# z in the order q, k, v, with q and k normalised behind products, and w_out and b1 prepared on other engines

## The chip, the cores and the metric

One core of a Trainium2 chip runs the whole layer in one launch. The metric is the device time of that launch in microseconds. The engines named below are TensorE (PE, with its weight loads as PEld), VectorE (DVE), ScalarE (ACT), GpSimd (POOL) and SyncE (SP, which here issues most of the loads).

## What is computed

One hybrid layer on 512 tokens of width 1024. A projection `z = h @ w_in` feeds three branches, and a mixture of experts follows. Cut to what the change touches:

```python
h = rms_norm(x, norm1_g) * (1 + sc1) + sh1
z = h @ w_in
xr, xg, q, k, v, qi, ki, wi = jnp.split(z, ...)
y_rnn = rg_lru_branch(xr, xg, ...)                 # conv, gates, scan, gelu(xg) * h
q = rms_norm(q.reshape(B, S, 8, 64), q_norm_g)     # each head by itself
k = rms_norm(k.reshape(B, S, 8, 64), k_norm_g)
y_attn = dsa_attention(q, k, v, qi, ki, wi)        # indexer scores, top keys, softmax, product with v
mix = jnp.concatenate([rms_norm(y_rnn, rg_out_g), rms_norm(y_attn, attn_out_g)], -1) @ w_out
x = x + g1 * mix
h2 = rms_norm(x, norm2_g) * (1 + sc2) + sh2
x = x + g2 * moe_ffn(h2, ...)                      # top 4 of 32 experts; u = h2 @ w1[e] + b1[e], then w2[e]
```

All weights are float32. Each expert has 1024 x 2048 numbers in w1 and 1024 x 1024 in w2.

## The kernel before, in words

Dense products of float32 are made of three passes: an operand is split into a high part (ScalarE casts it to the reduced format, L152) and a low part (VectorE or POOL subtracts the high part, L153), and TensorE adds high x high, low x high and high x low (L157 to L159). A matrix of w_in is loaded in eight row blocks of 512 columns; `halves` splits and multiplies it in two halves. The last argument of `halves` and `tok_piece` is the engine that makes the low parts, VectorE if none is given. A product of four groups of tokens gives 24 records of 256 columns a group; two PSUM banks take turns, and ScalarE empties each (L293 for token-major results, L306 for xg).

The order of the stages around the change is: xr and xg of the recurrent branch, whose gates and four scans over 512 tokens run on ScalarE, POOL and VectorE (L399 a square root, L402, L403 the scan, L400 gelu, L404); k; k's norm (squares on ScalarE L454, sums L455, the inverse root by twelve small VectorE instructions, L141 to L148); v; `prep_k` (L462 scales k by its norm, L468 transposes it); w_out's first half with `split_out` (L491 multiplies its rows by g1r, the gate of the residual; L492 and L493 make high and low parts); q; the first four of eight products of the recurrent branch with w_out (`rg`); q's norm and `prep_q` (L553 scales, L475 transposes); then `attend`, four blocks of queries with pieces of other work handed in `between`. While VectorE still picks the top keys in rounds of two instructions (L361, L362), the z products run. The bias b1 of the experts is split into three parts of bf16 after `attend(3)`, on POOL (L680 to L686), for a product with one row that adds it in the expert stage. Behind attention and the second half of w_out the router sorts tokens, and a loop over experts streams w1 and w2 (1 MB a load, L823) from HBM, multiplies (L884, L911) and adds the rows to the output.

Memory is laid out by hand: R[0] to R[5] are regions of on-chip memory that weights, then other data, take in turn, so a load waits until the last reader of the region is done. Each engine runs its own list of instructions in order. Who comes first on each list is not written by hand: a list scheduler sorts the instructions by its own estimates of durations, once, when the kernel is built. The source order sets priorities.

Of the kernel before, what the change touches and what calls it, by code (L numbers as in the profile page):

```python
# [9 lines left out]
F32R = mybir.dt.float32r  # L10
BF = mybir.dt.bfloat16
# [26 lines left out]
def layer(ctx, tc, x, c, w_ada, b_ada, norm1_g, w_in, conv_w, conv_b, w_rg_a, b_rg_a, w_rg_x, b_rg_x,  # L38
# [148 lines left out]
    def load_in(kb, c0, n=512):  # L187
        return pair(kb, KD, n, 2, lambda t, ks: nc.sync.dma_start(t, wi_v[:, ks, c0:c0 + n]))
# [95 lines left out]
    def halves(piece, t, evac, sub=None):  # L284
        for a in range(2):
            piece(part_of(t, 256 * a, 256 * a + 256), *evac(a), sub)
# [149 lines left out]
    load_bd()  # L436
    w_xg = load_in(R[2], 512)
    halves(ch_piece, w_xr, lambda a: (ev_xr, 2 * a), G)
    w_k = load_in(R[0], 1536)
    modulate(1)  # L440
    for b in range(4):
        rg_in(b)
    halves(ch_piece, w_xg, lambda a: (ev_xg, 2 * a), G)
    rg_out()
    w_v = load_in(R[1], 2048, 256)
    dump("gx", gx)
    dump("xr", xrp)
    dump("yR", yR)
# [37 lines left out]
    def split_out(a, kb, g):  # L486

        raw, low = wo[a]
        hi = mem(kb, 4, D, dt=F32R)
        for b in range(4):  # L490
            G.tensor_mul(raw[b][:, 0], raw[b][:, 0], g1r)  # L491
            A.activation(hi[:, b], raw[b][:, 0], AF.Copy, scale=g(b))  # L492
            V.scalar_tensor_tensor(low[b][:, 0], raw[b][:, 0], g(b), hi[:, b], op0=OP.mult, op1=OP.subtract)  # L493
        return hi, [v[:, 0] for v in low]

    ssA = const.tile([128, NT], F32)
    mh, ml = mem(R[3] + 8, 4, S, dt=F32R), mem(R[4], 4, S, dt=F32R)

    def rg_half():
        p = bank(7)  # L500
        sq = mem(R[4] + 8, 4, S)
        for b in range(4):
            A.activation(sq[:, b], yR[:, b], AF.Square)
            T.matmul(p[32 * b:32 * b + 32, :], ones, sq[:, b], start=True, stop=True)
        V.tensor_copy(sq[:, 0], p)
        p = bank(7)
        for i in range(NT):
            T.matmul(p[:, i:i + 1], sq[:, 0, i * 128:(i + 1) * 128], fold[:, 0:1], start=True, stop=True)
        V.tensor_copy(ssA, p[:, 0:NT])
        r = rstd_of(ssA, 512, "rs1")  # L510
        for b in range(4):
            hilo(mh[:, b], ml[:, b], yR[:, b])
        wh, wl = split_out(0, R[1], grg)
        return r, wh, wl

    def rg_out_half(i, n, r, wh, wl):
        p = bank(0, 1, 2, 3)
# [3 lines left out]
            mm3(p, mh[:, b, sl], ml[:, b, sl], wh[:, b, ns], wl[b][:, ns], b, 4)  # L521
        V.scalar_tensor_tensor(part[:, i, ns], p, r[:, i:i + 1], part[:, i, ns], op0=OP.mult, op1=OP.add)  # L522


    halves(tok_piece, w_k, lambda a: (ev_tok(zk, 256 * a),), G)
    rk = norm_heads(zk, "k", 191, rls)
    tok_piece(w_v, ev_tok(zv, 0))
    for pr in range(4):
        prep_k(pr, rk)
    w_q = load_in(R[2], 1024)  # L530
    wo_v = w_out[0].rearrange("(b p) n -> p b n", p=128)
    wo = [None, None]

    def load_wo(a):
        wo[a] = pair(R[2 * a], 4, D, 1, lambda t, bs: nc.sync.dma_start(t, wo_v[:, 4 * a + bs.start:4 * a + bs.stop]))

    load_wo(0)
    rows_of(g1r, 0)
    brt = const.tile([128, E], F32)
    nc.sync.dma_start(brt, at(b_router, 0, [[0, 128], [1, E]]))  # L540
    nc.sync.dma_start(wrt, w_router[0].rearrange("(p k) e -> p k e", k=KD))
    half_a = rg_half()
    halves(tok_piece, w_q, lambda a: (ev_tok(zq, 256 * a),))
    for i in range(NT):
        nc.sync.dma_start(part[:, i], x[0, i * 128:(i + 1) * 128, :])
    load_wo(1)
    rg = [partial(rg_out_half, i, n, *half_a) for i in (3, 2, 1, 0) for n in range(2)]
    for f in rg[0:4]:
        f()
    rq = norm_heads(zq, "q", 191.5, [mem(174.75 + 2 * j, S) for j in range(2)])  # L550
    for i in range(NT):
        z = zq[:, i].rearrange("p (h d) -> p h d", h=H)
        (G if i % 2 else V).tensor_mul(z, z, rq[:, i, :, None].to_broadcast([128, H, HD]))  # L553
    for pr in range(4):
        prep_q(pr)


    natt = [0]
# [50 lines left out]
    def mix_in(i):  # L609

        y = yB[:, i]
        ssB = const.tile([128, 1], F32, name="ssB", tag="ssB", bufs=2)
        A.activation(sqB, y, AF.Square, accum_out=ssB)
        r = rstd_of(ssB, 512, "rB")
        bh, bl = [mem(R[3] + 2 * j, 4, 128, dt=F32R) for j in range(2)]
        p = bank(4, 5).rearrange("p (b t) -> p b t", b=4)
        for b in range(4):
            T.transpose(p[:, b], y[:, b * 128:(b + 1) * 128], ident)
        hilo(bh, bl, p)
        return bh, bl, r  # L620
# [48 lines left out]
    V.tensor_sub(upto_me, onesb, later)  # L669
    attend(3, rg[4:6])  # L670
    half_b = split_out(1, R[5], gat)

    b1t = const.tile([96, 2 * FF], BF)
    for n in range(2):
        ns = slice(n * FF, (n + 1) * FF)
        b1f = mem(R[3] + 4, FF)
        for j in range(3):
            nc.sync.dma_start(b1f[32 * j:32 * j + 32], b1[0, :, ns])
        b1o = b1f[0:96].rearrange("p (f two) -> p f two", two=2)[:, :, 1]
        G.tensor_scalar(b1o, b1o, 1.0, None, op0=OP.add)  # L680
        G.tensor_copy(b1t[:, ns], b1f[0:96])
        for j in range(1, 3):
            for q in range(j, 3):
                c = slice(32 * q, 32 * q + 32)
                G.tensor_sub(b1f[c], b1f[c], b1t[c, ns])
                G.tensor_copy(b1t[c, ns], b1f[c])  # L686
    m3 = mix_in(3)
    attend(2, rg[6:7] + [partial(mix_half, 3, n, *m3, *half_b) for n in range(2)])
    m2 = mix_in(2)
# [395 lines left out]
```

## Time and profile before

| | us |
|---|---|
| median of 3 runs | 1457.71 (1455.44 to 1466.08) |
| profiled execution | 1457.75 |
| its span on the core | 1455.9 |
| TensorE busy | 1363.4, 94% of the span |
| VectorE busy | 547.6, 38% |
| ScalarE busy | 273.3, 19% |
| POOL busy | 204.1, 14% |
| HBM moved | 482.39 MB |

The span is what the hardware profiler saw of the core's instructions; the time of the execution is 1.85 us longer. The granted clock of TensorE is given as a share of full speed, 2.4 GHz; the other level is 1.2 GHz, 0.50. Matmuls are pipelined: a record's duration is longer than the distance to the next. An idle time in brackets stands ahead of an instruction, with what ended it.

### The profile page before, as it was taken

To read this page: it belongs to the slowest core of one execution; us is meant where nothing else is said; L and a number is where in the kernel's file an instruction comes from. 1 tells how busy PE (TensorE), PEld (TensorE's weight loads), DVE (VectorE), ACT (ScalarE), POOL (GpSimd) and SP (SyncE) were. 2 spreads that over 40 slices of the span, in tenths; PEclk is the share of its full clock that TensorE was granted. 3 is DMA by queue.
4 is the path that set the end of the run, shared out by engine and by line. 5 is a ranking of instruction groups with operands and counts; after the bars stand their busy time and mean duration, and the time that the engine had idled before them with its cause. 6 is when DMAs were issued, how large, how long until landed. Compare 5 with 4: busy or idle time off the path is not lost. (4 is left out here: it accounts for less than half of the span.)

```text
span 1455.9 us, 26502 instructions
## 1 busy us (share of the span) xinstructions
PE 1363.4 (94%) x10907; PEld 611.4 (42%) x10907; DVE 547.6 (38%) x1317; ACT 273.3 (19%) x552; POOL 204.1 (14%) x238
## 2 busy tenths in 40 slices
PE   5999988999799999999999999999999999999993
PEld 2854887767533343334333333333333333333320
DVE  4579986755722222214212231223132122212221
ACT  4445553433111100101011000001010010100100
POOL 4312623511100010000001011000000000100000
PEclk9999999878689999999999999999999999999997
DMA  9676113014999999999999999999999999999995
GB/s 373 219 270 231 59 59 117 22 58 159 374 390 363 323 404 392 391 407 404 409 395 403 418 401 383 402 410 389 410 399 404 409 405 407 399 393 393 395 418 197
DMA packets 83398, 482.39 MB, mean 331 GB/s; under 512 B 11778, under 2 KB 14018, under 8 KB 33098
## 3 DMA queue, kind: packets, MB, share of 16 engines
q1 hardware_dynamic: 75034, 453.88, 77.8%
q0 software_dynamic: 7520, 24.68, 6.7%
q8 instruction: 87, 1.43, 0.4%
q10 hardware_dynamic: 720, 2.10, 0.4%
q14 instruction: 37, 0.30, 0.1%
HBM read 465.14 MB, written 15.48 MB: 330 GB/s over the span
## 5 line engine op out<-in xcount | busy, mean ns | idle before, releaser
L884 PE MATMUL bank<-mem,mem 128*32 128x512 f32 x5504 | 622.4, 595 | 0.0
L884 PEld LDWEIGHTS bank<-mem,mem 128*32 128x32 f32 x5504 | 174.6, 110 | 371.6 <-issue 363.2
L911 PE MATMUL bank<-mem,mem 128*32 128x512 f32 x2304 | 268.4, 593 | 0.0
L889 DVE TENSOR_TENSOR bank<-bank,mem 128x512 f32<-128x512 f32 x86 | 60.0, 697 | 410.1 <-PE bank L884 409.8
L911 PEld LDWEIGHTS bank<-mem,mem 128*32 128x32 f32 x2304 | 85.0, 110 | 146.0 <-issue 134.1
L891 ACT ACTIVATE mem<-bank 128x256 f32<-128x256 f32 x86 | 33.1, 385 | 527.8 <-DVE bank L889 527.8
L930 DVE SCALAR_TENSOR_TENSOR mem<-bank,gate_h,mem 64x512 f32<-64x512 f32 x72 | 54.0, 749 | 207.2 <-PE bank L911 206.5
L933 POOL DMA_INDIRECT out_dram<-mem,idx_all x32 | 47.0, 1470 | 581.7 <-DVE mem L930 525.9
L157 PE MATMUL bank<-mem,mem 128*128 128x512 f32 (+1 forms) x320 | 115.0, 362 | 2.9 <-DVE mem L522 2.3
L158 PE MATMUL bank<-mem,mem 128*128 128x512 f32 (+1 forms) x320 | 113.7, 355 | 0.0
L159 PE MATMUL bank<-mem,mem 128*128 128x512 f32 (+1 forms) x320 | 112.7, 352 | 0.0
L855 POOL DMA_INDIRECT mem<-h_d,idx_all x32 | 30.2, 943 | 400.4 <-PE bank L863 342.7
L157 PEld LDWEIGHTS bank<-mem,mem 128*128 128x128 f32 x320 | 62.3, 196 | 14.3 <-issue 3.5
L159 PEld LDWEIGHTS bank<-mem,mem 128*128 128x128 f32 x320 | 62.4, 195 | 12.9 <-issue 6.8
L917 PE MATMUL bank<-mem,mem 128*32 128x512 f32 x448 | 61.8, 601 | 6.0 <-SPq L1014 4.3
L158 PEld LDWEIGHTS bank<-mem,mem 128*128 128x128 f32 x320 | 62.6, 195 | 9.3 <-issue 3.5
L864 DVE COPY mem<-bank 128x512 f32<-128x512 f32 (+2 forms) x32 | 18.0, 564 | 112.5 <-PE bank L863 112.2
L863 PEld LDWEIGHTS bank<-ident,mem 128*128 128x128 f32 (+2 forms) x256 | 33.7, 196 | 58.7 <-issue 26.8
L902 ACT COPY mem<-bank 128x512 f32<-128x512 f32 (+1 forms) x32 | 18.3, 573 | 207.9 <-PE bank L911 115.3
L863 PE MATMUL bank<-ident,mem 128*128 128x128 f32 (+2 forms) x256 | 43.6, 295 | 11.2 <-ACT mem L902 5.1
L153 POOL TENSOR_TENSOR mem<-mem,mem 128x512 fp32r<-128x512 f32 (+1 forms) x28 | 41.2, 1490 | 86.4 <-ACT mem L152 86.3
L901 PEld LDWEIGHTS bank<-ident,mem 128*128 128x128 f32 x172 | 24.5, 207 | 37.5 <-issue 21.1
(325 smaller groups left out, 1216.9 us busy)
## 6 DMA issues: line engine op xcount, KB each, us to landing
mem<-in_w_dram SPq DMA_DIRECT2D x384, 1024.0 KB, 15.1
mem<-in_w_ada_dram SPq DMA_DIRECT2D x24, 1024.0 KB, 6.3
mem<-in_w_in_dram SPq DMA_DIRECT2D x20, 512.0 KB, 5.5
mem<-in_x_dram SPq DMA_DIRECT2D x8, 512.0 KB, 6.4
mem<-in_w_out_dram SPq DMA_DIRECT2D x8, 512.0 KB
mem<-in_w_in_dram SPq DMA_DIRECT2D x8, 256.0 KB, 5.9
mem<-mod_d SPq DMA_DIRECT2D x4, 512.0 KB, 6.0
h_d<-mem POOLq DMA_DIRECT2D x4, 512.0 KB, 8.6
```

What stands on the lines that cost most here:

```text
L153: (sub or V).tensor_sub(lo, src, hi)
L157: T.matmul(p, ah, bh, start=(k == 0), stop=False)
L158: T.matmul(p, al, bh, start=False, stop=False)
L159: T.matmul(p, ah, bl, start=False, stop=(k == n - 1))
L863: T.transpose(p[:, k, 0:n], xgs[frm][0:n, 4 * q + k::KD], ident[0:n, 0:n])
L884: T.matmul(bk[b][32 * n:32 * n + 32, :], xT[:, k, BT * b:BT * b + BT], w[k][:, 0, n * 512:(n + 1) * 512], start=(k == 0), stop=(k == KD - 1))
L889: V.tensor_add(bk[b], bk[b], biasb[j % 2])
L891: A.activation(act[:, b], u[:, :, 0], AF.Gelu_apprx_sigmoid)
L911: T.matmul(bk[6 + b // 2][o:o + 32, :], aT[:, b, c, BT * n:BT * n + BT], w[n][:, c, m * 512:(m + 1) * 512], start=(n + c == 0), stop=(n == ...
L917: T.matmul(bk[6 + nb // 2][o:o + 32, :], aT[:, nb - 1, c, BT * n:BT * n + BT], w[n][:, c, m * 512:(m + 1) * 512], start=(n == 0), stop=(n ...
L930: V.scalar_tensor_tensor(ys[64 * h:64 * h + a.stop - a.start, ns], p[a], gate_h[a, h, j:j + 1], g2h[a], op0=OP.mult, op1=OP.mult)
L933: G.indirect_dma_start(out=out_rows, out_offset=bass.IndirectOffsetOnAxis(ap=idx_all[a, j:j + 1], axis=0), in_=ys[a], in_offset=None, comp ...
```

## The change

Four things are altered. The z products come in the order q, k, v: w_q takes R[0], w_k R[1] and w_v R[2], and POOL makes the low parts of all three. q's norm and its product with z follow q's product, all on VectorE; k's product is cut in two halves, with `prep_q` and the recurrent branch's sums of squares around its second half; k's norm stands ahead of v's product, and `prep_k` behind it. In `split_out` the rows of w_out are multiplied by g1r on VectorE in place of POOL. And b1 is split ahead of k's norm by `split_b1`, with VectorE and ScalarE, in a piece of memory of its own; `mh` and the buffers `bh`, `bl` change places in R[3].

```diff
--- before.py
+++ after.py
@@ -436,13 +436,14 @@
     load_bd()
     w_xg = load_in(R[2], 512)
     halves(ch_piece, w_xr, lambda a: (ev_xr, 2 * a), G)
-    w_k = load_in(R[0], 1536)
+    w_q = load_in(R[0], 1024)
     modulate(1)
     for b in range(4):
         rg_in(b)
+    w_k = load_in(R[1], 1536)
     halves(ch_piece, w_xg, lambda a: (ev_xg, 2 * a), G)
     rg_out()
-    w_v = load_in(R[1], 2048, 256)
+    w_v = load_in(R[2], 2048, 256)
     dump("gx", gx)
     dump("xr", xrp)
     dump("yR", yR)
@@ -488,13 +489,13 @@
         raw, low = wo[a]
         hi = mem(kb, 4, D, dt=F32R)
         for b in range(4):
-            G.tensor_mul(raw[b][:, 0], raw[b][:, 0], g1r)
+            V.tensor_mul(raw[b][:, 0], raw[b][:, 0], g1r)
             A.activation(hi[:, b], raw[b][:, 0], AF.Copy, scale=g(b))
             V.scalar_tensor_tensor(low[b][:, 0], raw[b][:, 0], g(b), hi[:, b], op0=OP.mult, op1=OP.subtract)
         return hi, [v[:, 0] for v in low]
 
     ssA = const.tile([128, NT], F32)
-    mh, ml = mem(R[3] + 8, 4, S, dt=F32R), mem(R[4], 4, S, dt=F32R)
+    mh, ml = mem(R[3], 4, S, dt=F32R), mem(R[4], 4, S, dt=F32R)
 
     def rg_half():
         p = bank(7)
@@ -510,8 +511,7 @@
         r = rstd_of(ssA, 512, "rs1")
         for b in range(4):
             hilo(mh[:, b], ml[:, b], yR[:, b])
-        wh, wl = split_out(0, R[1], grg)
-        return r, wh, wl
+        return r
 
     def rg_out_half(i, n, r, wh, wl):
         p = bank(0, 1, 2, 3)
@@ -521,38 +521,61 @@
             mm3(p, mh[:, b, sl], ml[:, b, sl], wh[:, b, ns], wl[b][:, ns], b, 4)
         V.scalar_tensor_tensor(part[:, i, ns], p, r[:, i:i + 1], part[:, i, ns], op0=OP.mult, op1=OP.add)
 
-
-    halves(tok_piece, w_k, lambda a: (ev_tok(zk, 256 * a),), G)
-    rk = norm_heads(zk, "k", 191, rls)
-    tok_piece(w_v, ev_tok(zv, 0))
-    for pr in range(4):
-        prep_k(pr, rk)
-    w_q = load_in(R[2], 1024)
+    b1t = const.tile([96, 2 * FF], BF)
+
+    def split_b1():
+
+        for n in range(2):
+            ns = slice(n * FF, (n + 1) * FF)
+            b1f = mem(161.75, FF)
+            for j in range(3):
+                nc.sync.dma_start(b1f[32 * j:32 * j + 32], b1[0, :, ns])
+            b1o = b1f[0:96].rearrange("p (f two) -> p f two", two=2)[:, :, 1]
+            V.tensor_scalar(b1o, b1o, 1.0, None, op0=OP.add)
+            A.copy(b1t[:, ns], b1f[0:96])
+            V.tensor_sub(b1f[0:96], b1f[0:96], b1t[:, ns])
+            for q in (1, 2):
+                c = slice(32 * q, 32 * q + 32)
+                A.copy(b1t[c, ns], b1f[c])
+            V.tensor_sub(b1f[64:96], b1f[64:96], b1t[64:96, ns])
+            A.copy(b1t[64:96, ns], b1f[64:96])
+
+
     wo_v = w_out[0].rearrange("(b p) n -> p b n", p=128)
     wo = [None, None]
 
     def load_wo(a):
         wo[a] = pair(R[2 * a], 4, D, 1, lambda t, bs: nc.sync.dma_start(t, wo_v[:, 4 * a + bs.start:4 * a + bs.stop]))
 
-    load_wo(0)
+
+    halves(tok_piece, w_q, lambda a: (ev_tok(zq, 256 * a),), G)
     rows_of(g1r, 0)
     brt = const.tile([128, E], F32)
     nc.sync.dma_start(brt, at(b_router, 0, [[0, 128], [1, E]]))
     nc.sync.dma_start(wrt, w_router[0].rearrange("(p k) e -> p k e", k=KD))
-    half_a = rg_half()
-    halves(tok_piece, w_q, lambda a: (ev_tok(zq, 256 * a),))
+    load_wo(0)
+    rq = norm_heads(zq, "q", 191.5, rls)
+    for i in range(NT):
+        z = zq[:, i].rearrange("p (h d) -> p h d", h=H)
+        V.tensor_mul(z, z, rq[:, i, :, None].to_broadcast([128, H, HD]))
+    k_half = lambda a: tok_piece(part_of(w_k, 256 * a, 256 * a + 256), ev_tok(zk, 256 * a), G)
+    k_half(0)
+    for pr in range(4):
+        prep_q(pr)
+    r_a = rg_half()
+    k_half(1)
+    half_a = (r_a, *split_out(0, R[1], grg))
+    split_b1()
+    rk = norm_heads(zk, "k", 191, rls)
+    tok_piece(w_v, ev_tok(zv, 0), G)
     for i in range(NT):
         nc.sync.dma_start(part[:, i], x[0, i * 128:(i + 1) * 128, :])
     load_wo(1)
+    for pr in range(4):
+        prep_k(pr, rk)
     rg = [partial(rg_out_half, i, n, *half_a) for i in (3, 2, 1, 0) for n in range(2)]
     for f in rg[0:4]:
         f()
-    rq = norm_heads(zq, "q", 191.5, [mem(174.75 + 2 * j, S) for j in range(2)])
-    for i in range(NT):
-        z = zq[:, i].rearrange("p (h d) -> p h d", h=H)
-        (G if i % 2 else V).tensor_mul(z, z, rq[:, i, :, None].to_broadcast([128, H, HD]))
-    for pr in range(4):
-        prep_q(pr)
 
 
     natt = [0]
@@ -612,7 +635,7 @@
         ssB = const.tile([128, 1], F32, name="ssB", tag="ssB", bufs=2)
         A.activation(sqB, y, AF.Square, accum_out=ssB)
         r = rstd_of(ssB, 512, "rB")
-        bh, bl = [mem(R[3] + 2 * j, 4, 128, dt=F32R) for j in range(2)]
+        bh, bl = [mem(R[3] + 8 + 2 * j, 4, 128, dt=F32R) for j in range(2)]
         p = bank(4, 5).rearrange("p (b t) -> p b t", b=4)
         for b in range(4):
             T.transpose(p[:, b], y[:, b * 128:(b + 1) * 128], ident)
@@ -669,21 +692,6 @@
     V.tensor_sub(upto_me, onesb, later)
     attend(3, rg[4:6])
     half_b = split_out(1, R[5], gat)
-
-    b1t = const.tile([96, 2 * FF], BF)
-    for n in range(2):
-        ns = slice(n * FF, (n + 1) * FF)
-        b1f = mem(R[3] + 4, FF)
-        for j in range(3):
-            nc.sync.dma_start(b1f[32 * j:32 * j + 32], b1[0, :, ns])
-        b1o = b1f[0:96].rearrange("p (f two) -> p f two", two=2)[:, :, 1]
-        G.tensor_scalar(b1o, b1o, 1.0, None, op0=OP.add)
-        G.tensor_copy(b1t[:, ns], b1f[0:96])
-        for j in range(1, 3):
-            for q in range(j, 3):
-                c = slice(32 * q, 32 * q + 32)
-                G.tensor_sub(b1f[c], b1f[c], b1t[c, ns])
-                G.tensor_copy(b1t[c, ns], b1f[c])
     m3 = mix_in(3)
     attend(2, rg[6:7] + [partial(mix_half, 3, n, *m3, *half_b) for n in range(2)])
     m2 = mix_in(2)
```

The orders of the engines, as the scheduler fixes them, are shown at three places. A row is line, operation, written and read tiles, shape, and in brackets the engines or DMA queues whose semaphores it waits for. The first place is ScalarE from an eviction of xg on: `bank_65` and `bank_66` are the two PSUM banks, `mem_85` takes xg, `mem_77` (before) and `mem_76` (changed) take k and q, `mem_1745` is the piece of b1. Before:

```order
L306 COPY mem_85<-bank_65 128x512 [waits PE_49]
L152 CAST mem_527<-mem_159 128x512 [waits PE_49,Pool_49]
L152 CAST mem_527<-mem_161 128x512 [waits PE_49,Pool_49]
L152 CAST mem_527<-mem_105 128x512 [waits PE_49,Pool_49]
L306 COPY mem_85<-bank_66 128x512 [waits PE_49]
L152 CAST mem_527<-mem_106 128x512 [waits Pool_49]
L400 ACT_TABLE_LOAD
L400 ACTIVATE mem_85<-mem_85 128x4x512 [waits Activation_49]
L293 COPY mem_77<-bank_65 128x256 [waits DMAHW5_49,DMAHW7_49,DMAHW2_49,PE_49]
L293 COPY mem_77<-bank_66 128x256 [waits PE_49]
```

And in the changed kernel:

```order
L306 COPY mem_85<-bank_65 128x512 [waits PE_49]
L152 CAST mem_527<-mem_159 128x512 [waits PE_49,Pool_49]
L152 CAST mem_527<-mem_161 128x512 [waits PE_49,Pool_49]
L539 CAST b1t<-mem_1745 32x1024 [waits DVE_49]
L152 CAST mem_527<-mem_105 128x512 [waits PE_49,Pool_49]
L539 CAST b1t<-mem_1745 32x1024
L306 COPY mem_85<-bank_66 128x512 [waits PE_49]
L152 CAST mem_527<-mem_106 128x512 [waits Pool_49]
L400 ACT_TABLE_LOAD
L400 ACTIVATE mem_85<-mem_85 128x4x512 [waits Activation_49]
L293 COPY mem_76<-bank_65 128x256 [waits DMAHW7_49,DMAHW2_49,PE_49]
L541 CAST b1t<-mem_1745 32x1024 [waits DVE_49]
```

Two copies of b1's parts (L539), the first of which waits for VectorE, now stand between the last two evictions of xg, and a third (L541) behind q's first eviction. The second place is VectorE around the scans of the recurrent branch, in the changed kernel:

```order
L362 MATCH_REPLACE mem_91<-m_627,mem_91 128x512 [waits DVE_49]
L403 SCALAR_TENSOR_TENSOR mem_78<-mem_85,mem_631 128x512 [waits DMAHW7_49,Pool_49]
L403 SCALAR_TENSOR_TENSOR mem_78<-mem_85,mem_631 128x512 [waits Pool_49] x3
L536 TENSOR_TENSOR mem_1745<-mem_1745,b1t 96x1024 [waits Activation_49]
L362 MATCH_REPLACE mem_91<-m_624,mem_91 128x384 [waits DVE_49]
L361 MAX m_626<-mem_91 128x8 [waits DVE_49]
L361 MAX m_625<-mem_91 128x8 [waits DVE_49]
L362 MATCH_REPLACE mem_91<-m_626,mem_91 128x512 [waits DVE_49]
L362 MATCH_REPLACE mem_91<-m_625,mem_91 128x384 [waits DVE_49]
L361 MAX m_627<-mem_91 128x8 [waits DVE_49]
L540 TENSOR_TENSOR mem_1745<-mem_1745,b1t 32x1024 [waits Activation_49]
```

The difference of b1 (L536), for which the first L539 waits, stands behind all four scans; L540 stands six rows further back. The third place is VectorE after q's last square in the changed kernel, where `saq` are the sums of squares, `mem_1432` holds the inverse root, `mem_76` is q and `mem_104` is g1r:

```order
L456 TENSOR_REDUCE saq<-mem_89 128x8 [waits Activation_49]
L492 TENSOR_TENSOR mem_159<-mem_159,mem_104 128x1024 [waits DMAHW5_49,PE_49,Pool_49]
L456 TENSOR_REDUCE saq<-mem_90 128x8 [waits Activation_49]
L492 TENSOR_TENSOR mem_161<-mem_161,mem_104 128x1024 [waits DMAHW6_49,PE_49,Pool_49]
L141 TENSOR_SCALAR mem_1432<-saq 128x32 [waits DVE_49]
L143 TENSOR_SCALAR mem_1432<-mem_1432 128x32 [waits DVE_49]
L492 TENSOR_TENSOR mem_105<-mem_105,mem_104 128x1024 [waits DMAHW7_49,PE_49,Pool_49]
L144 TENSOR_SCALAR mem_1432<-mem_1432 128x32 [waits DVE_49]
L146 SCALAR_TENSOR_TENSOR mem_1432<-mem_1432 128x32 [waits DVE_49]
L147 TENSOR_TENSOR mem_1432<-mem_1432 128x32 [waits DVE_49]
L492 TENSOR_TENSOR mem_106<-mem_106,mem_104 128x1024 [waits DMAHW0_49,PE_49,Pool_49]
L148 SCALAR_TENSOR_TENSOR mem_1432<-mem_1432 128x32 [waits DVE_49]
```

Four products of w_out's rows (L492), each of which waits for a DMA and for POOL, stand among the instructions of the norm. In the kernel before, these products were on POOL and the norm's instructions followed one another.

## Rows read from the trace of the kernel before

**Rows 1.** The page, part 1: busy us, share of the span, instructions.

```profile
PE 1363.4 (94%) x10907; PEld 611.4 (42%) x10907; DVE 547.6 (38%) x1317; ACT 273.3 (19%) x552; POOL 204.1 (14%) x238
```

**Rows 2.** Stretches: busy us of each engine, granted clock, DMA share, GB/s.

```profile
148.00:199.00 51.00, 50.74 (x356) 47.09 (x354) 44.51 (x71) 28.22 (x46) 33.05 (x20) 1.00 0.24 83
199.00:208.00 9.00, 5.65 (x31) 4.85 (x31) 8.70 (x24) 4.84 (x7) 0.00 (x0) 0.81 0.01 2
248.00:264.00 16.00, 11.04 (x31) 6.43 (x30) 13.06 (x17) 6.18 (x9) 7.58 (x4) 0.68 0.00 2
290.00:310.00 20.00, 16.48 (x55) 12.35 (x55) 10.05 (x18) 3.31 (x9) 6.93 (x5) 0.58 0.00 1
410.00:1455.00 1045.00, 997.13 (x8914) 343.60 (x8906) 262.12 (x592) 98.72 (x208) 74.29 (x61) 0.99 0.99 390
```

**Rows 3.** Waits of SyncE's queue, 300 to 450: total us, times, longest.

```profile
SPq L823 <- PE bank L587: 34.6, 1, 34.6
```

**Rows 4.** Timeline of VectorE: start, us, line, tiles, [idle before].

```profile
196.32 2.33 DVE L146 SCALAR_TENSOR_TENSOR mem<-mem 128x32 f32<-128x32 f32 x1
198.68 0.19 DVE L147 TENSOR_TENSOR mem<-mem 128x32 f32<-128x32 f32 x1
...
200.49 1.76 DVE L462 TENSOR_TENSOR mem<-mem,mem 128x256 f32<-128x256 f32 x5
```

**Rows 5.** Timeline of POOL.

```profile
163.55 8.13 POOL L153 TENSOR_TENSOR mem<-mem,mem 128x512 fp32r<-128x512 f32 x5
...
189.14 9.46 POOL L491 TENSOR_TENSOR mem<-mem,mem 128x1024 f32<-128x1024 f32 x4 [12.74 <-DMA mem<-in_w_out_dram]
...
287.34 4.35 POOL L685 TENSOR_TENSOR mem<-mem,b1t 32x1024 f32<-32x1024 f32 x2
```

**Rows 6.** Timeline of TensorE, 248 to 262.

```profile
249.25 0.33 PE L475 MATMUL bank<-ident,mem 128*128 128x128 f32 x1 [1.07 <-DVE mem L553]
...
254.64 0.80 PE L157 MATMUL bank<-mem,mem 128*128 128x512 f32 x1 [2.28 <-DVE mem L522]
```

**Rows 7.** Timelines of VectorE and TensorE, 284 to 302.

```profile
289.72 1.98 DVE L146 SCALAR_TENSOR_TENSOR rB<-rB 128x1 f32<-128x1 f32 x1
...
294.06 0.90 PE L587 MATMUL bank<-ident,mem 128*128 128x128 f32 x3 [2.46 <-ACT mem L582]
```

**Rows 8.** Timelines of ScalarE and VectorE, 150 to 186.

```profile
154.71 1.92 ACT L399 ACTIVATE mem<-mem 128x2048 f32<-128x2048 f32 x1
...
164.01 0.59 ACT L306 COPY mem<-bank 128x512 f32<-128x512 f32 x1 [0.72 <-PE bank L159]
165.79 0.62 ACT L152 CAST mem<-mem 128x512 fp32r<-128x512 f32 x1 [1.19 <-POOL mem L153]
...
158.03 8.81 DVE L403 TENSOR_TENSOR_SCAN mem<-mem,mem 128x512 f32<-128x512 f32 x4 [0.20 <-POOL mem L402]
...
170.63 0.68 DVE L362 MATCH_REPLACE8 mem<-m,mem 128x512 f32<-128x512 f32 x1
```

**Rows 9.** Timeline of TensorE at the first z records of 256 columns.

```profile
163.81 0.28 PE L157 MATMUL bank<-mem,mem 128*128 128x256 f32 x1
163.93 0.27 PE L158 MATMUL bank<-mem,mem 128*128 128x256 f32 x1
```

**Rows 10.** Instructions of L492, L493 (ns min/median/max); timelines, 150 to 186.

```profile
L492 ACT ACTIVATE mem<-mem,svt x8: 1137/1140/1152, 203.9 to 264.3; 128x1024 fp32r<-128x1024 f32 x8
L493 DVE SCALAR_TENSOR_TENSOR mem<-mem,svt,mem x8: 1276/1280/2598, 211.5 to 274.2; 128x1024 fp32r<-128x1024 f32 x8
173.10 0.37 ACT L293 COPY mem<-bank 128x256 f32<-128x256 f32 x1 [2.93 <-PE bank L159]
179.27 0.63 ACT L454 ACTIVATE mem<-mem 128x512 f32<-128x512 f32 x1
...
176.60 2.48 DVE L153 TENSOR_TENSOR mem<-mem,mem 128x512 fp32r<-128x512 f32 x4
...
179.94 0.69 DVE L455 TENSOR_REDUCE sak<-mem 128x8 f32<-128x512 f32 x1 [0.85 <-ACT mem L454]
```

## The prediction, made before the changed kernel was run

> **What bounds the kernel now.** I read the page's first part, then a table of stretches, then the waits of SyncE's queue, and last the timelines of the engines around the stretches in which TensorE stands. TensorE is busy for 94% of the span [rows 1]. From 410 to 1455 us TensorE is busy for 997 of 1045 us at a granted clock of 0.99, with a DMA share of 0.99: the expert stage is bound by both [rows 2]. Its weights do not start on their own. SyncE's first weight load waits 34.6 us for TensorE's transposes at L587, which belong to attention [rows 3]. So what is gained or lost before about 320 us moves the weight stream and with it the end, nearly one for one. I take 1 for 1.
>
> Before 320 us TensorE is the engine that decides, and three stretches stand out. The work that a stretch does at full clock is its busy time times the granted clock; the rest of it is lost. That gives 9 - 5.65 x 0.81 = 4.4 us in 199 to 208, 16 - 11.04 x 0.68 = 8.5 us in 248 to 264, and 20 - 16.48 x 0.58 = 10.4 us in 290 to 310, in all **23.3 us** [rows 2]. In each the engine first waits, and then runs for some microseconds between the two clocks of 2.4 and 1.2 GHz. In 148 to 199, where xg's, k's and v's products run one behind the other, nothing is lost: 50.74 of 51 us at 1.00 [rows 2].
>
> **What the change takes away.** (1) 199 to 208. TensorE has ended the products and waits for k's norm. Its rstd chain on VectorE takes 2.33 us at 196.32 for an instruction of 128x32, where the next eight take 0.22 from start to start [rows 4], and this just while POOL's four L491 (w_out's rows times g1r) run from 189.14 to 198.60 [rows 5]. In the changed order k's norm stands behind q's k_half(1) product and ahead of w_v's 96 records, which at 0.12 us from start to start [rows 9] cover 11.5 us; L491 is no longer on POOL. I take the 4.4 us as gained. (2) 248 to 264. TensorE waits 1.07 us for L553 (z times r of q) and 2.28 us for L522, which VectorE comes to late [rows 6]; q's norm is now made long before attention, so 8.5 us go with it. (3) 290 to 310. rB's small instructions, 128x1, take 1.98 us [rows 7] beside POOL's L685 [rows 5]; the custom instruction L581 comes late behind them, ScalarE's L582 behind that, and TensorE's L587 waits 2.46 us for L582 [rows 7]. The b1 parts leave POOL and this place, so 10.4 us go. What is late next in each of them I can't see; the 23.3 us are an upper end, and 15 (two thirds) the lower one.
>
> **What the change adds.** b1's parts are made in the z stage, one half after the other, by a chain that crosses between VectorE and ScalarE: L534, copy L535, difference L536, two copies L539, difference L540, copy L541 (lines of the changed code, as all below that I give as "new"). The scheduler's order puts L536 on VectorE behind the four scans L403, and on ScalarE the first L539, which waits for L536, ahead of the eviction L306 of xg's last block. Step by step: ScalarE's square root L399 ends at 156.6 [rows 8] and stands one cast of 0.62 us later in the new order [rows 8], so 157.2. The scans follow POOL's products on it, from 158.03 now, from about 158.65 then, and take 8.81 us [rows 8]: 167.5. L536 is 96x1024 with two inputs; no row has it, and the nearest on VectorE is L493, 128x1024, 1.28 us [rows 10]: 168.7. L539 and L541, 32x1024, are nearest to L492 on ScalarE, 128x1024, 1.14 us [rows 10]: 169.9. A cast of 0.62 us and the second L539 follow, 171.6, and L306's 0.59 us [rows 8]: 172.2. TensorE's z records of 256 columns begin at 163.8, where xg's product is at its end, and its first q group of 24 records lasts 2.88 us [rows 9], so from 166.7 on it needs the bank that L306 empties. It waits **5.5 us** where it waits for nothing now. Were L539 priced by a cast of 128x512, 0.62, it would be 4.5; were L536 2.6, the longest L493, 6.8.
>
> After a wait the clock falls: the three stretches lost 1.1, 3.5 and 6.9 us to it (busy time times one minus the granted clock) [rows 2]. For one wait of 5.5 us I take 3, nearest to the second, with 1 and 7 as ends. The second half of b1 crosses the engines again between the evictions of q's fourth to sixth group; each eviction is 0.37 us [rows 10] and a group 2.88, so there is room, and I take 0.8 us for both crossings (0 to 3). **q's product ends 9.3 us later.**
>
> q's norm is then on the path, since k_half(0) with its 96 records (11.5 us) is all that stands ahead of prep_q's transposes. From the end of q's last group: eviction 0.37, square 0.63, reduction 0.69 us [rows 10], twelve small instructions at 0.22 from start to start, 2.7 [rows 4], the four products z times r (new L560) at about 0.7 for 128x512, 2.7, and in between, now on VectorE, w_out's products with g1r (new L492): four, 128x1024 with two inputs, at L493's 1.28 [rows 10], 5.1. That makes 12.2, and some 13.4 with the evictions that ScalarE has to do in between: 1.9 us after TensorE is ready. POOL's L153 run beside it, and by what L491 did to the rstd chain [rows 4, 5] some of the 20 instructions will take a POOL instruction's time. I take **3.5 us** with the clock (0 to 10). Smaller waits for evictions behind VectorE's part of prep_q (new L481), **1.2 us** (0 to 3). k's norm and prep_k stand behind w_v's product with some 4 us to spare: nothing. The low parts of w_v and w_q go from VectorE, 2.48 us for four [rows 10], to POOL at 1.63 each [rows 5]; POOL is idle enough between (33 of 51 us busy [rows 2]) and ahead of TensorE by more than a group, so nothing by itself. SyncE's queue gets b1's six loads ahead of w_out's and x's; none of those is waited for within 10 us after it: nothing. VectorE gains w_out's eight products and loses the low parts, about even.
>
> The sum: -23.3 + 9.3 + 3.5 + 1.2 = **-9.3 us**. The profiled execution took 1457.75 us, span 1455.9 and 1.85 around it, and equals the median of the runs, 1457.71. So 1457.7 - 9.3 = **1448.4 us**.
>
> **What speaks most against it.** VectorE's rstd chain was slow exactly while POOL's four L491 ran: 2.33 us for one instruction, beside 2.37 for one L491 [rows 4, 5]. The Trainium skill, "SBUF — State Buffer", section "SBUF: two separate sides", says that VectorE and GpSimd arbitrate for one port pair as an exclusive lock: a VectorE instruction in a two-port mode, or with two SBUF inputs, and a GpSimd one keep it for their whole length, and the other blocks. By that rule the trace's 2.33 us are VectorE blocked by L491, and moving w_q's and w_v's low parts to POOL brings back what moving L491 takes away. It is the third rival below.
>
> **The rivals.** (a) *The wait at 166.7 does not come*, because L536 finds its place before the evictions matter. Against it stands the order itself, which is fixed; for it, that all five steps of the chain are priced from other shapes, and that the scans may start earlier. Then -23.3 + 3.5 + 1.2 = -18.6 us, **1439** (1434 to 1443).
> (b) *Slower*: TensorE stays at 1.2 GHz through the rest of q's product. After the first wait seven groups of 2.88 us are left, which take twice that; each crossing of b1's second half then lets it wait again before the clock is back. 20.2 us in place of the 3 taken gives 1448.4 + 17.2 = **1466**. For it: 290 to 310 stayed at 0.58 for 20 us, with two waits of 2.46 and less [rows 2, 7]. Against it: evictions have 2.5 us to spare in each group, more at the half clock. It decides if TensorE waits again within the two or three groups after the first wait.
> (c) *VectorE's products wait out POOL's.* The four new L492 and four new L560 ahead of prep_q each wait for one L153 of 1.63 us [rows 5], 13 us in place of 3.5: 1448.4 + 9.5 = **1458**. Against it: VectorE's L362 took no more than 0.68 us beside POOL's five L153 of 163 to 172 [rows 5, 8], though it has one large input and new L492 has two.
>
> **How the numbers follow.** Forecast 0.45, (a) 0.31, (b) 0.12, (c) 0.12. The time is that of the forecast, 1448.4; its own range is 1442 to 1455 (the ends of the terms do not fall together). The range of 8 in 10 reaches from (a)'s lower end, 1434, to 1464, inside (b). One per cent is 14.6 us, about what a measurement of this kernel can tell from no change: faster is below 1443.1, slower above 1472.3. Faster: nearly all of (a) and a sixth of the forecast, 0.35. Slower: (b) with more waits than priced, 0.08. The rest, 0.57, lies within.
>
> **What would show it.** In the profile after: no wait of TensorE for the products of k with its norm, for those of q or for L582's successor in attention, and a granted clock of 0.9 and more in the two stretches that answer to 248 to 264 and 290 to 310; a wait of TensorE of about 5 to 6 us for L306 or ScalarE near 167 with the clock below 1 behind it; q's product ending near 196 (it would be 187 without the wait); TensorE waiting 1 to 4 us for VectorE at the first transpose of prep_q; and the first weight load of the expert stage some 9 us earlier. The prediction is wrong if the wait near 167 is missing or above 9 us, if attention keeps stretches below 0.7, or if the expert stage, 410 to 1455, changes its own length by more than 3 us.

## The result and the profile after

The changed kernel took 1447.01 us (median of 10 runs, 1445.29 to 1450.13) where the kernel before took 1459.22 on the same chip (10 runs, 1455.44 to 1466.08): 0.9923 of before, 95% interval 0.9910 to 0.9937. Forecast were 1448.4 us and -9.3; measured are -12.2 by the medians, and -8.8 between the two profiled executions (1457.75 and 1448.97). The changed kernel's page, parts 1 and 2:

```profile
PE 1354.4 (94%) x10907; PEld 607.8 (42%) x10907; DVE 541.7 (37%) x1321; ACT 280.6 (19%) x560; POOL 175.5 (12%) x224
PEclk9999999998699999999999999999999999999997
```

TensorE has 9 us less of busy time than in [rows 1]. Where the time came from is read in a table of stretches of the changed kernel, columns as in [rows 2]:

```profile
166.00:178.00 12.00, 5.89 (x30) 5.68 (x29) 11.92 (x24) 8.72 (x10) 6.49 (x5) 0.72 0.32 111
199.00:208.00 9.00, 8.60 (x72) 8.39 (x70) 8.69 (x17) 3.45 (x7) 3.84 (x3) 1.00 0.22 90
206.00:220.00 14.00, 9.60 (x52) 6.62 (x50) 10.95 (x13) 4.86 (x8) 5.41 (x4) 0.76 0.01 2
248.00:264.00 16.00, 15.90 (x73) 11.44 (x71) 15.48 (x25) 8.29 (x12) 0.00 (x0) 1.00 0.30 118
290.00:310.00 20.00, 20.00 (x106) 15.68 (x106) 7.78 (x25) 7.58 (x21) 0.00 (x0) 0.91 0.00 1
410.00:1447.00 1037.00, 987.30 (x8822) 341.31 (x8814) 262.17 (x592) 98.56 (x208) 74.12 (x61) 0.99 0.99 389
```

The three stretches of [rows 2] that lost 23.3 us now lose 0.4, 0.1 and 1.8 (length less busy time times clock): 21.0 us are gone. Two new stretches have come, 166 to 178 with 12 - 5.89 x 0.72 = 7.8 us and 206 to 220 with 14 - 9.60 x 0.76 = 6.7 us. The clock of a long stretch is a mean over idle time too. The same formula, summed over stretches of 2 us, gives 8.9 and 7.7 for these two, and 4.8, 9.0 and 11.1 us for what the kernel before lost in 198 to 208, 248 to 264 and 290 to 312. Where a loss is given below without its product, it is summed in this finer way. TensorE's longest waits between 140 and 330 name both:

```profile
PE bank L157 <- ACT mem L306: 6.1, 1, 6.1
PE bank L476 <- DVE mem L560: 4.1, 2, 2.8
PE bank L157 <- ACT mem L293: 1.0, 2, 0.6
```

The first is the wait that the order foretold. VectorE's timeline, then ScalarE's, then TensorE's:

```profile
166.81 2.21 DVE L536 TENSOR_TENSOR mem<-mem,b1t 96x1024 f32<-96x1024 f32 x1
...
169.05 1.04 ACT L539 CAST b1t<-mem 32x1024 bf16<-32x1024 f32 x1 [7.63 <-DVE mem L536]
...
171.83 0.59 ACT L306 COPY mem<-bank 128x512 f32<-128x512 f32 x1
...
172.47 0.58 PE L157 MATMUL bank<-mem,mem 128*128 128x256 f32 x1 [6.11 <-ACT mem L306]
```

L536 comes behind the scans, ScalarE stands 7.63 us for it, and the eviction L306 is over at 172.4. The second new stretch, VectorE and POOL:

```profile
205.94 0.19 DVE L146 SCALAR_TENSOR_TENSOR mem<-mem 128x32 f32<-128x32 f32 x1
206.16 1.23 DVE L147 TENSOR_TENSOR mem<-mem 128x32 f32<-128x32 f32 x1
207.43 1.19 DVE L148 SCALAR_TENSOR_TENSOR mem<-mem 128x32 f32<-128x32 f32 x1
208.66 4.56 DVE L560 TENSOR_TENSOR mem<-mem,mem 128x512 f32<-128x512 f32 x4
...
206.05 5.41 POOL L153 TENSOR_TENSOR mem<-mem,mem 128x512 fp32r<-128x512 f32 x4 [5.16 <-ACT mem L152]
```

The last two instructions of the norm take 1.2 us each, where the one ahead takes 0.19, and the four products with z 4.56 us, from the moment at which POOL starts on w_k's second half. The first weight load of the expert stage, SyncE's timeline of before, then of after:

```profile
321.79 2.04 SPq L823 DMA_DIRECT2D mem<-in_w_dram  x4
```

```profile
312.04 1.92 SPq L831 DMA_DIRECT2D mem<-in_w_dram  x4
```

It goes out 9.75 us earlier, and the span ends 8.7 us earlier (1455.9 and 1447.2): what the dense part gains does arrive. Two executions of the changed kernel differ by about 3 us from this load on (1447.2 - 312.0 and, on another chip, 1442.7 - 310.6), and the profiled executions of all kernels here take 1132 to 1137 us from it to the end, so a microsecond or two in that stage is not explained here.

### The profile page after: what moved, and what is told of

The parts are those of the page before. It is cut to its first block, busy times and chain, and to the rows that moved or that the text cites. A ratio compares the mean times of both kernels' runs of the same rounds, so it can differ in the third digit from the quotient of the medians.

```text
span 1447.2 us, 26470 instructions
## 1 busy us (share of the span) xinstructions
PE 1354.4 (94%) x10907; PEld 607.8 (42%) x10907; DVE 541.7 (37%) x1321; ACT 280.6 (19%) x560; POOL 175.5 (12%) x224
## 5 line engine op out<-in xcount | busy, mean ns | idle before, releaser
L153 POOL TENSOR_TENSOR mem<-mem,mem 128x512 fp32r<-128x512 f32 (+1 forms) x40 | 59.7, 1510 | 102.6 <-ACT mem L152 102.5
```

The lines of the kernel that those rows point to most:

```text
L153: (sub or V).tensor_sub(lo, src, hi)
```

## The experiments

All were timed against before, four kernels to a chip, with 4 to 6 runs each and 11 of before. The change stood at 0.9923 above. Repeated on the chip of the squares behind q, of b1 done twice and of w_out's products on VectorE, it stood at 0.9932.

| kernel | median us | of before, 95% |
|---|---|---|
| after, again | 1448.1 | 0.9932, 0.9915 to 0.9950 |
| b1's copies behind the gelu | 1444.7 | 0.9922, 0.9905 to 0.9940 |
| w_out's products behind q's norm | 1448.3 | 0.9943, 0.9925 to 0.9961 |
| both | 1446.4 | 0.9928, 0.9909 to 0.9947 |
| after, b1 late, VectorE and ScalarE | 1439.0 | 0.9882, 0.9853 to 0.9910 |
| after, b1 late, POOL | 1439.6 | 0.9886, 0.9860 to 0.9913 |
| the same, done twice | 1442.8 | 0.9901, 0.9885 to 0.9916 |
| b1 late, w_out's products behind the sums | 1431.4 | 0.9824, 0.9794 to 0.9854 |
| that, and the squares behind q | 1428.5 | 0.9795, 0.9780 to 0.9810 |
| before, b1 on VectorE and ScalarE | 1445.8 | 0.9930, 0.9912 to 0.9948 |
| before, w_out's products on VectorE | 1441.1 | 0.9873, 0.9857 to 0.9890 |
| before, both moves | 1434.9 | 0.9856, 0.9829 to 0.9882 |

The theory: the gain comes from POOL's work being taken from beside VectorE's small instructions; the new costs come from b1's chain in the z stage and from w_out's products among q's norm. `issue_after` below queues what is written under it, on the same engine, behind an instruction; it adds no wait. Every edit also lets the list scheduler sort anew, so a time alone does not separate the engine from the order; the durations of the same instructions do.

**b1's copies behind the gelu.**

```diff
-    split_b1()
+    with tc.issue_after(gelu.ins):
+        split_b1()
```

> The changed kernel, with ScalarE's copies of b1's parts queued behind the gelu, so that none stands ahead of an eviction of xg. Theory: the wait of 6.1 us of TensorE for the eviction L306 at 166 us and the half clock behind it (8.9 us lost in 166 to 178) go, and up to 1 us comes back where the copies stand between q's evictions: 7 to 9 us less than the changed kernel's 1447, so 1438 to 1440, ratio to before 0.986. Rival: the chain of b1 is what costs, wherever it stands; then q's evictions wait for it in the later groups and the time stays within 3 us of 1447.

No difference that can be measured in the time: 0.9922. In the profiled execution the first weight load goes out at 307.4, 3 to 5 us ahead of the change's 312.0 and 310.6, so a gain of that size is not excluded. The wait for L306 is gone, and others have come. TensorE's waits of this kernel, 150 to 330:

```profile
PE bank L157 <- ACT mem L293: 5.1, 3, 3.9
PE bank L477 <- DVE mem L561: 5.0, 1, 5.0
```

A copy of b1 now waits for VectorE ahead of an eviction of q (3.9 us at one place), and q's norm is 5.0 us late in place of 4.1. The rival was nearer: the chain costs wherever it stands between evictions.

**w_out's products behind q's norm.**

```diff
-    half_a = (r_a, *split_out(0, R[1], grg))
+    with tc.issue_after(zr.ins):      # zr: the last product of z and r
+        half_a = (r_a, *split_out(0, R[1], grg))
```

> The changed kernel, with VectorE's four products of w_out's rows with g1r queued behind q's norm and its product with z. Theory: they are what made q's norm late (5 us in its chain, the first of them waiting for a DMA); without them the norm ends before POOL's low parts of w_k's second half begin at 206 us, TensorE's two waits of 2.8 and 1.3 us and the clock behind them (7.3 us lost in 207 to 220) go: 5 to 7 us less than 1447, so 1440 to 1442. Rival: VectorE is held by POOL's low parts; then q's products with z still take 1.15 us each, and at most 3 us are gained.

A miss: 0.9943, no gain. The trace gives the theory its first half, VectorE's timeline:

```profile
202.59 2.49 DVE L560 TENSOR_TENSOR mem<-mem,mem 128x512 f32<-128x512 f32 x4
205.01 6.82 DVE L492 TENSOR_TENSOR mem<-mem,mem 128x1024 f32<-128x1024 f32 x4
...
214.49 0.69 DVE L506 COPY mem<-bank 128x512 f32<-128x512 f32 x1
```

The products with z (L560) are back to 2.49 us and TensorE no longer waits for them. But the four L492, 6.82 us, now stand ahead of L506, the copy of the recurrent branch's summed squares, and TensorE's L509 waits 3.4 us for it.

**Both.** The two edits together.

```diff
+    with tc.issue_after(zr.ins):
+        half_a = (r_a, *split_out(0, R[1], grg))
+    with tc.issue_after(gelu.ins):
+        split_b1()
```

> Both orders at once: b1's copies behind the gelu and w_out's products behind q's norm. Theory: the two costs are separate and add, 12 to 16 us less than 1447, so 1431 to 1435, ratio to before 0.982. Rival: with the first wait gone q's norm comes earlier and meets b1's second half and POOL's low parts of w_k, so that the sum is at most 9 us.

0.9928: nothing added. TensorE waits 4.9 us for q's evictions and 6.2 us for that copy. Taking one wait away uncovered the next in the same in-order list.

**Before, with b1 on VectorE and ScalarE at the old place.** The body of the split is replaced by the changed kernel's, nothing else:

```diff
-        G.tensor_scalar(b1o, b1o, 1.0, None, op0=OP.add)
-        G.tensor_copy(b1t[:, ns], b1f[0:96])
...
+        V.tensor_scalar(b1o, b1o, 1.0, None, op0=OP.add)
+        A.copy(b1t[:, ns], b1f[0:96])
...
```

> The kernel before, with b1's parts made by VectorE and ScalarE in place of POOL, at the old place behind the first block of attention. Theory: POOL's instructions held VectorE's small ones there; with POOL free the 10.4 us lost in 290 to 310 go, less 1 to 3 us for VectorE's four differences of 1.25 us in attention: 7 to 10 us less than before's 1459, ratio 0.994. Rival: the place is what costs, because attention's chain has no room for this work on VectorE and ScalarE either; then the time stays within 3 us of before or rises.

0.9930, 10.8 us less: about as much as the whole change. Stretch 290 to 310, and one of rB's instructions on VectorE:

```profile
290.00:310.00 20.00, 20.00 (x114) 15.38 (x113) 12.10 (x36) 12.03 (x26) 0.00 (x0) 1.00 0.08 24
...
288.76 0.16 DVE L146 SCALAR_TENSOR_TENSOR rB<-rB 128x1 f32<-128x1 f32 x1
```

Nothing is lost there at clock 1.00, and the instruction that took 1.98 us in [rows 7] takes 0.16. At this place the engine was the cost, not the place.

**The changed kernel, b1 late, on VectorE and ScalarE.** `split_b1()` moves behind `attend(3)`, its buffer from 161.75 to R[3] + 12:

```diff
-    split_b1()
     rk = norm_heads(zk, "k", 191, rls)
...
     half_b = split_out(1, R[5], gat)
+    split_b1()
```

> The changed kernel, with b1's parts on VectorE and ScalarE, but behind the first block of attention, where the kernel before had them. Theory: b1's chain in the z stage costs 9 us and more, because its steps stand in ScalarE's list ahead of evictions and wait for VectorE; in attention the same work costs next to nothing (there it left 0 to 1 us lost). So the z stage loses no more than 1 us up to q's end, q's norm stays late by 5 us, and the time is 6 to 9 us below 1447: 1438 to 1441. Rival: q's product ended earlier only moves the waits to q's norm and to the recurrent branch's squares, as with the copies behind the gelu: 1444 to 1447.

1439.0, as the theory said: 0.9882 against 0.9923 and 0.9932 of the change, 6 to 7 us. TensorE's wait for q's norm stays at 4.0 us, and 160 to 178 still loses 1.6 us to another wait, for an eviction of q at 172.

**The same late place, on POOL.**

```diff
-            V.tensor_scalar(b1o, b1o, 1.0, None, op0=OP.add)
-            A.copy(b1t[:, ns], b1f[0:96])
...
+            G.tensor_scalar(b1o, b1o, 1.0, None, op0=OP.add)
+            G.tensor_copy(b1t[:, ns], b1f[0:96])
...
```

> The changed kernel, with b1's parts on POOL again, behind the first block of attention. Theory: POOL's instructions hold VectorE's small ones there as in the kernel before, 10 us lost in attention, against 9 gained in the z stage: 1446 to 1450, and 7 to 10 us above the kernel with b1 late on VectorE and ScalarE. Rival: it was the order of the parts that hurt in the kernel before, and with q and k prepared earlier attention has room for POOL's work: 1438 to 1441.

1439.6: the theory's 1446 to 1450 missed. POOL at the end of its work, and rB's chain on VectorE:

```profile
247.49 1.76 POOL L534 TENSOR_SCALAR mem<-mem 96x512 f32<-96x512 f32 x1 [44.80 <-DMA mem<-in_b_dram]
...
277.13 1.03 POOL L540 CAST b1t<-mem 32x1024 bf16<-32x1024 f32 x1
...
276.33 0.15 DVE L141 TENSOR_SCALAR rB<-ssB 128x1 f32<-128x1 f32 x1 [0.33 <-ACT mem L633]
278.41 0.16 DVE L146 SCALAR_TENSOR_TENSOR rB<-rB 128x1 f32<-128x1 f32 x1
```

POOL starts at 247 and is done at 278.2, just after rB's chain begins at 276.3; 250 us to the first weight load loses nothing. In the kernel before it started at 268 and went on to 297, over the chain, and 290 to 312 lost 11.1 us. There b1's buffer lies over z of q, and its load waited 14.2 us for q's transposes (L475); here it lies over z of k, and waits 5.7 us for L463, so the new order and the buffer's place both bear on the earlier start. So it is the overlap that costs, and not POOL's work in attention as such.

**Done twice**, so that POOL works on through the chain.

```diff
-        for n in range(2):
+        for n in (0, 1, 0, 1):
```

> The changed kernel with b1's parts on POOL behind the first block of attention, and the whole splitting done twice (the second time writes the same numbers), so that POOL works on through the stretch in which rB's small instructions run. Theory: POOL's instructions on memory hold VectorE's small ones; without the doubling they were over when rB's chain began (278 us), with it they stretch that chain to 1 to 2 us an instruction, TensorE waits for L602's successor and loses 6 to 11 us: 1446 to 1450 against 1439.6. Rival: the chain was late in the kernel before for its place in VectorE's order; then rB's instructions stay at 0.15 us and the time within 3 us of 1439.6.

1442.8, 0.9901 against 0.9886: 2 to 3 us, where 6 to 11 were expected, and the intervals overlap. Both timelines:

```profile
280.31 0.90 DVE L146 SCALAR_TENSOR_TENSOR rB<-rB 128x1 f32<-128x1 f32 x1
281.25 0.16 DVE L147 TENSOR_TENSOR rB<-rB 128x1 f32<-128x1 f32 x1
281.44 1.98 DVE L148 SCALAR_TENSOR_TENSOR rB<-rB 128x1 f32<-128x1 f32 x1
...
281.29 4.32 POOL L539 TENSOR_TENSOR mem<-mem,b1t 32x1024 f32<-32x1024 f32 x2
```

The mechanism shows (1.98 us for an instruction of 0.16 beside POOL's L539), but the second round began at 278.5 and only the chain's last instructions met it; 250 to 300 lost 3.5 us where the single round lost none. So the trace shows the mechanism and the time does not. That the loss grows with how much of the chain is met fits 0, 3.5 and 11.1 us in three kernels; it was not varied further.

**w_out's products behind the sums**, with b1 late on VectorE and ScalarE.

```diff
+    with tc.issue_after(ssc[0].ins):      # ssc: the copy of the recurrent branch's sums to ssA
+        half_a = (r_a, *split_out(0, R[1], grg))
```

> The same, and VectorE's products of w_out's rows queued behind the copy of the recurrent branch's sums, that is behind all that k_half's stretch needs from VectorE. Theory: the three places at which VectorE's or ScalarE's list made TensorE wait (166, 207, and 212 where the products stood ahead of that copy) are all free; 7 us more off, 1431 to 1435, ratio to before 0.983. Rival: w_out's high and low parts then come late for the first product with w_out, and TensorE waits there instead; at most 3 us off the kernel with b1 late.

1431.4, as expected; 7.6 us less than with b1 late alone on the same chip. The products with z on VectorE:

```profile
194.83 0.19 DVE L148 SCALAR_TENSOR_TENSOR mem<-mem 128x32 f32<-128x32 f32 x1
195.06 2.50 DVE L562 TENSOR_TENSOR mem<-mem,mem 128x512 f32<-128x512 f32 x4
```

2.50 us where the change has 4.56: q's norm now ends before POOL starts on w_k's second half (198.88), and nobody waits for it.

**Before, both moves.** b1 on VectorE and ScalarE at the old place, and `V.tensor_mul` for w_out's rows; z in the old order.

```diff
-            G.tensor_mul(raw[b][:, 0], raw[b][:, 0], g1r)
+            V.tensor_mul(raw[b][:, 0], raw[b][:, 0], g1r)
...
-        G.tensor_scalar(b1o, b1o, 1.0, None, op0=OP.add)
+        V.tensor_scalar(b1o, b1o, 1.0, None, op0=OP.add)
...
```

> The kernel before, z in its old order, with b1's parts on VectorE and ScalarE at the old place and w_out's products on VectorE. Theory: k's norm is no longer held by POOL's products; of the 4.4 us lost in 199 to 208 and of the 5 in 248 to 260 about 4 to 6 go, less what the products cost VectorE itself: 3 to 6 us below the kernel with b1 alone moved (1445.8): 1440 to 1443. Rival: VectorE's own products stand in k's norm as POOL's held it, and the time stays at 1445 to 1448.

1434.9, better than expected: 0.9856, 21 us by the ratio. So the two moves of engine alone give nearly twice what the change gives, with z in its old order.

**Before, w_out's products on VectorE.** This is one line.

```diff
-            G.tensor_mul(raw[b][:, 0], raw[b][:, 0], g1r)
+            V.tensor_mul(raw[b][:, 0], raw[b][:, 0], g1r)
```

> The kernel before with one edit: w_out's products with g1r on VectorE in place of POOL. Theory: moving b1 alone gave 10.8 us and both moves 21 to 23, so this one alone gives 9 to 12, ratio 0.993. Rival: the two moves help each other, since POOL is empty only with both; then 3 to 6 us.

0.9873, 18 us, where 9 to 12 were expected, so the two moves overlap (11 and 18 alone, 21 together). `split_out` runs twice, so the line moves eight products. VectorE's timeline at k's norm and at rB's chain, and POOL:

```profile
192.98 0.18 DVE L141 TENSOR_SCALAR mem<-sak 128x32 f32<-128x32 f32 x1
193.20 0.18 DVE L143 TENSOR_SCALAR mem<-mem 128x32 int32<-128x32 int32 x1
193.30 1.23 DVE L491 TENSOR_TENSOR mem<-mem,mem 128x1024 f32<-128x1024 f32 x1
...
279.54 1.81 DVE L147 TENSOR_TENSOR rB<-rB 128x1 f32<-128x1 f32 x1
...
276.99 4.34 POOL L685 TENSOR_TENSOR mem<-mem,b1t 32x1024 f32<-32x1024 f32 x2
```

The norm's instructions are at 0.18 us even with the products, 1.23 us each, in between. The second four products are what [rows 6] does not show. In the kernel before, VectorE and POOL at q's norm and behind it:

```profile
239.55 2.15 DVE L141 TENSOR_SCALAR mem<-saq 128x32 f32<-128x32 f32 x1
241.74 2.33 DVE L143 TENSOR_SCALAR mem<-mem 128x32 int32<-128x32 int32 x1
...
251.57 2.35 DVE L669 TENSOR_TENSOR mem<-onesb,later 128x128 bf16<-128x128 bf16 x1 [0.93 <-POOL mem L553]
...
239.28 4.76 POOL L491 TENSOR_TENSOR mem<-mem,mem 128x1024 f32<-128x1024 f32 x2 [40.67 <-DMA mem<-in_w_out_dram]
...
251.50 4.67 POOL L491 TENSOR_TENSOR mem<-mem,mem 128x1024 f32<-128x1024 f32 x2
```

Two of q's small instructions took over 2 us there, and L669, ahead of the L522 that TensorE waited 2.28 us for, took 2.35; without POOL's L491 they take 0.17, 0.17 and 0.22. With this one line 248 to 264 loses 0.7 us in place of 9.0, with q's norm still ahead of attention. rB's chain still meets POOL (1.81 us), but b1's splitting starts 12 us earlier, at 256.4, and 264 to the first weight load loses 5.9 us in place of 11.1. That accounts for 5 of the 8 us by which the two moves overlap.

**The squares behind q**, on top of the fastest.

```diff
-    r_a = rg_half()
+    with tc.issue_after(evq.ins):      # evq: q's last eviction
+        r_a = rg_half()
```

> The fastest so far (b1 late on VectorE and ScalarE, w_out's products behind the recurrent branch's sums), and ScalarE's squares of that branch queued behind q's last eviction, since they wait for POOL's L404 ahead of an eviction that TensorE waits 1.6 us for at 172. Theory: that wait goes, 1.5 to 2 us off, ratio to before 0.981. Rival: the squares come late for the sums and w_out's products behind them, and nothing is gained.

1428.5, the lowest of all: 0.9795, some 30 us below before and 20 below the change. Its interval overlaps that of the kernel it builds on, whose first weight load goes out at 295.4 where this one's does at 292.0. Its stretches:

```profile
166.00:178.00 12.00, 12.00 (x102) 12.00 (x102) 12.00 (x25) 5.56 (x11) 12.00 (x10) 1.00 0.01 3
206.00:220.00 14.00, 14.00 (x119) 14.00 (x118) 13.44 (x26) 9.95 (x16) 0.00 (x0) 1.00 0.01 1
306.00:322.00 16.00, 15.63 (x64) 13.55 (x64) 9.42 (x49) 6.11 (x19) 1.73 (x1) 0.57 0.07 28
```

From 150 to 300 TensorE loses about 1 us. What is left lies behind that: 306 to 322 runs at 0.57 with hardly any wait, and that was not looked into. The kernel before has such a stretch too: from 340 to 352 it is busy for 11.7 of 12 us, at 0.50 to 0.58.

**The change again**, beside the last three.

> The changed kernel once more, on the chip of these runs. Expected by every theory: 0.992 to 0.993 of before.

0.9932; its two waits are there again, 6.1 and 4.1 us.

## Why the prediction was right, step by step

*The expert stage follows the dense part one for one.* Right: 9.75 us at the first weight load, 8.7 at the end.

*What goes: 23.3 us.* Right in size (21.0 by the same formula), and right in cause for the first and the third stretch: POOL beside VectorE's small instructions. For 248 to 264 the cause was misread. The prediction put that gain down to the new order of z ("q's norm is now made long before attention"), and that was not needed: it is POOL's second L491 beside q's norm and L669, and the one line that moves them takes 9.0 us down to 0.7. Before with the two moves of engine, and with q's norm still ahead of attention, loses 3.6 us from 200 to 300 where before lost 19.2. The new order, with b1 out of the way and w_out's products behind the sums, may be worth 2 to 4 us more: 0.9824 against 0.9856 on one chip, with intervals that overlap, and 1.9 us by the first weight loads (295.4 and 297.3).

*b1's chain: 9.3 us.* Right: 6.1 us of wait where 5.5 were worked out, 8.9 us with the clock, and 0.4 for the second half. The walk through the order hit each instruction within a microsecond, in part by luck, since two errors had opposite signs: the scans began at 158.08 and not at 158.65, and L536 took 2.21 us and not 1.28, beside POOL's two L153 of 163.59 to 167.93. At the end of the kernel it was worth less, 6 to 7 us (b1 late): with b1 away, a wait for q's eviction at 172 still costs 1.6 us.

*q's norm: 3.5 us.* Mis-sized: 7.7 us in the stretch, 7.6 by the run. The prediction took the length of the chain to decide (1.9 us late) and some of POOL's work on top. VectorE's timeline of the changed kernel:

```profile
197.65 2.09 DVE L492 TENSOR_TENSOR mem<-mem,mem 128x1024 f32<-128x1024 f32 x1 [2.66 <-DMA mem<-in_w_out_dram]
...
200.26 1.72 DVE L492 TENSOR_TENSOR mem<-mem,mem 128x1024 f32<-128x1024 f32 x1
```

The chain comes late, first for w_out's DMA (2.66 us ahead of the first L492), then because these two L492 stand beside POOL's low parts and take 2.09 and 1.72 us, where the next two take 1.23: 1.4 us. So its end meets POOL's low parts of w_k's second half, 1.0 + 1.0 us for two small instructions and 2.1 for the products with z: 5.5 us are POOL's in all. So rival (c) was part of the truth, at 5.5 us in place of 13. By the Trainium skill, "SBUF — State Buffer", section "SBUF: two separate sides", two inputs in on-chip memory are enough for an instruction of VectorE to be held by GpSimd; the trace agrees, 4.56 us for four beside POOL's work and 2.50 without.

*Smaller waits: 1.2 us.* About right: 1.0 for evictions (L293), of which 0.4 is the one above, and 0.2 for L469.

*The sum.* From 100 us to the first weight load, TensorE loses 30.7 us before and 23.9 after. That is 6.7 us less, where the terms of the prediction gave 9.3: q's norm costs 4 us more than its term, and small losses elsewhere are 1.5 us less, half of them ahead of 148 us, which the repeat of the change does not show again. The load moved by 9.75. The other 3.0 us are work that the prediction held equal: busy time times clock falls from 191.1 to 188.1 us. The four kernels here in the old order of z have 189.4 to 191.1 us of it up to that load, the ten in the new order 185.9 to 188.1. Most of the difference is the recurrent branch's sums of squares. TensorE's timeline of before, then of the kernel with w_out's products behind the sums, where the clock is 1.00 too:

```profile
217.57 1.56 PE L504 MATMUL bank<-mem,ones 128*32 128x512 f32 x4
...
219.49 1.05 PE L504 MATMUL bank<-mem,ones 128*32 128x512 f32 x2
...
221.13 1.05 PE L504 MATMUL bank<-mem,ones 128*32 128x512 f32 x2
```

```profile
201.23 1.07 PE L507 MATMUL bank<-mem,ones 128*32 128x512 f32 x8
```

In the old order of z the eight records stand in three pieces between products and hold TensorE for 3.4 us, each piece taken up to the start of the next product (1.49, 0.98 and 0.97); in the new order all eight follow one another and hold it for 1.0. So 2.4 of the 3.0 us are found, and the rest stays open. The total came near the mark partly by luck, with one term 4 us too low and a gain of 3 us unseen.

*The rivals.* (a) did not come: the order was kept. (b) did not come: TensorE was back at full clock by 178, and the groups after had room for the second half of b1 (one wait of 0.4 us). (c) in part.

## What to carry to other kernels

Before work is moved from GpSimd, look for small VectorE instructions that take 1 to 2 us instead of 0.2 beside it: here one line, moving eight products off GpSimd, gave 18 us where the whole change gave 12. Work that crosses two engines several times is better kept out of the list of an engine that empties PSUM; in a list in order everyone behind it waits for the slower partner, here 6.1 us. When one such wait is taken away, read the same list for the next instruction that someone waits for, and move the work behind that one too.

## What the runs showed that was not expected

The gains of two moves did not add: 11 and 18 us alone, 21 together. POOL's splitting of b1 cost 11 us or nothing, depending on a start 20 us earlier. And TensorE's clock fell without a wait of note: 306 to 322 of the fastest kernel has 15.63 of 16 us busy at 0.57.
